# Two slabs on the unnormalised input open each hybrid layer, and the bias tables move ahead of the first layer

## The chip, the cores and the metric

The kernel runs on one core of a Trainium2 chip. The metric is device time in microseconds (us) of one launch; the number that counts is the median over several runs. One execution was also recorded by the hardware profiler, and every row below comes from that execution. TensorE is called PE, VectorE DVE, ScalarE ACT, SyncE SP; SP issues most of the loads and computes nothing.

## What is computed

The program is two blocks over 256 tokens of width 1024. The first block has two hybrid layers (convolution, retention and windowed attention side by side), the second has two layers of a mixer and a mixture of experts. The change touches the openings of the two hybrid layers and one table of the mixers. What matters of the reference:

```python
def hybrid_layer(x, positions, norm_g, w_in, ...):
    h = rms_norm(x, norm_g)                  # x * rsqrt(mean(x*x) + EPS) * norm_g
    z = h @ w_in
    (c_glu, c_gate, r_q, r_k, r_v, r_gate, a_q, a_k, a_v, a_gate, g_logit) = jnp.split(z, offsets, axis=-1)
    y_conv = conv_module(c_glu, c_gate, ...) @ w_conv_out   # v = a * sigmoid(b); 31 taps; layer norm
    ...
def sliding_window_attention(q, k, v, sink, rel_bias):      # in the mixers
    bias = rel_bias.astype(jnp.float32)[t5_causal_bucket(dist)]
    logits = jnp.where(mask[None, :, None, None], logits + bias, NEG_INF)
```

The factor rsqrt(mean(x*x) + EPS) belongs to a token. It can therefore be multiplied into a product after the matrix multiplication: (x * norm_g) @ w, times the token's factor, equals h @ w.

## The kernel before

**Numbers in two parts.** Every large product is made of three passes in a fast 32-bit format. Each operand is split into a rounded part (hi, made by ACT) and the rest (lo, made by DVE), and PE adds hi*hi, hi*lo and lo*hi. `split` (L87) does this for activations and for weights.

**Slabs.** Weights come in slabs of 1024 x 256 numbers, 1 MB each. `half` (L101) loads half a slab (512 KB) on SP's queue into `raw`, and splits it into `hi` and `lo`; there are 4 raw, 5 hi and 5 lo buffers. One slab feeds 48 matmuls of 256 columns: `mm_T` (L118) with the weights stationary, `mm_R` (L129) with the activations stationary. In the trace both orders run on lines L125 to L127 or L135 to L137.

**Opening of a hybrid layer.** `Norm` (L174) first makes u = x * norm_g in two parts (`uh`, `ul`) and the sums of squares, then in `_end` (L202) the reciprocal root `rinv` (a chain of small DVE instructions, spread over the partitions by PE on L151), and then, for each of eight blocks kt of 128 channels, h = x * norm_g * rinv on DVE (L212), its hi part `h_hi` on ACT and its lo part `h_lo` on DVE (L88). The first slab of the layer does not wait for h: `conv_unit(c, uu)` (L402) multiplies u by the slab and applies `rinv` to the result (L406). How many slabs do this is `UNORM[l]`. Then comes the slab of the attention keys, "ak", on h (L573), then "av" and the rest in the order of `HYB_ORDER`. Convolution unit c needs one slab and then 31 DVE instructions (taps), which `after_slab` (L380) hands out, 3.5 for each slab; a new unit is started when the list of taps is empty.

**Hold.** When h for kt = 7 is traced, `_end` remembers the ACT and the DVE instruction (L221). Of the half slabs traced after it, numbers 5 to 12 have their splits put behind these two instructions on ACT and DVE (L107 to L110, `HOLD` = 2); numbers 1 to 4 have not.

**Bias tables.** `toeplitz` (L303) makes the eight rows of relative bias for the mixers: it loads `relb`, `oneh` and `outw` on SP, and for each head runs a matmul of 32 rows x 383 columns (L312, two passes), one DVE instruction (L314) and one store to `tb_dram`, issued by ACT (L315). It takes both buffers of ring S, three of ring O and the two banks "sc". The mixers read the stored rows after the hybrid layers. In the order of layer 0 it is the letter t, behind the retention projection R.

**The planner.** The kernel's text sets priorities, not the order itself. A planner simulates the program and gives each engine its list: at each step the ready instruction of the highest priority, which is the one traced earlier; `high_priority` moves the marked ones ahead. Each engine then runs its list strictly in that order, and a waiting instruction holds all that stand behind it.

Of the kernel before, what the change touches and what calls it, by code (L numbers as in the profile page):

```python
# [26 lines left out]
RET_H = 4  # L27
LEAD = 420
HYB_BUFS = {"A": 3, "Q": 4, "S": 2, "V": 1, "B": 2, "O": 3, "G": 2, "H": 2, "W": 1, "X": 3, "Y": 2}
HYB_ORDER = ("aaraarArrnRtggggC", "aaraarArrnRtggggC")  # L30
MIX_ORDER = "tKQRv012uh3b"
HOIST, P_FIRST = True, 2
PEER_NS, PEER_NI, AHEAD = 44, 12, 2
UNORM = (1, 1)
MIX_U, PEER_U = 1, 1
BANKS = {"mm": (0, 1, 2), "sc": (3, 4), "tr": (5, 6), "o": (7,), "xo": (7,), "xm": (0, 1, 2, 7), "pm": (0, 1), "g": (3, 4), "gy": (3, 4), "acc": (2, 5, 6, 7), "pb": (2,)}
PEER_ADA = (1, 4)
# [13 lines left out]
def two_blocks_kernel(ctx: ExitStack, tc: tile.TileContext, ins: dict, out: bass.AP, stages=None):  # L51
# [6 lines left out]
    def const(name, shape, dt=F32, src=None, pool=glob):  # L58
        t = pool.tile(shape, dt, tag=name, name=name, bufs=1)
        nc.sync.dma_start(t, ins[name] if src is None else src)  # L60
        return t
# [21 lines left out]
    def nm(base):  # L83
        uid[0] += 1
        return f"{base}_{uid[0]}"
# [7 lines left out]
    def bank(ring="mm", shape=(P, 2, T)):  # L93
        n = turns[ring] = turns.get(ring, -1) + 1
        b = BANKS[ring][n % len(BANKS[ring])]
        return psum.tile(list(shape), F32, tag=f"bank{b}", name=nm(ring))
# [156 lines left out]
    stages_m = [l for k, l in stages if k == "m"]  # L253
# [12 lines left out]
    ada = {l: [] for l in mods}  # L266
# [15 lines left out]
    def ada_units(l, pool, tag, bufs, size, place=None):  # L282
        cact = []

        def load():
            cp, ct = place or (pool, "c_rows")
            cact.append(cp.tile([P, D], F32, tag=ct, name=nm("c_rows"), bufs=1))
            nc.sync.dma_start(cact[0], ins["c_rows"])
            nc.scalar.activation(cact[0], cact[0], AF.Silu)

        yield load
        for j in range(48):
            for c in range(0, D, size):
                def unit(j=j, c=c):
                    w = pool.tile([P, size], F32, tag=tag, name=nm("ada"), bufs=bufs)
                    nc.sync.dma_start(w, ins["w_ada"][l, j, :, c:c + size])
                    t = pool.tile([P, 1], F32, tag="adt", name=nm("adt"))
                    nc.vector.scalar_tensor_tensor(w, w, 1.0, cact[0][:, c:c + size], op0=ALU.mult, op1=ALU.mult,  # L298
                                                   accum_out=t)
                    nc.vector.tensor_tensor(mods[l][:, j:j + 1], mods[l][:, j:j + 1], t, op=ALU.add)  # L300
                yield unit

    def toeplitz(pool):  # L303
        relb = pool.tile([P, 1024], F32, tag="S", name="relb", bufs=2)[:32].rearrange("p (h c) -> p h c", h=8)
        ow = pool.tile([P, 1024], F32, tag="S", name="ow", bufs=2)
        oneh, outw = ow[:32, 0:383], ow[:, 512:895]
        nc.sync.dma_start(relb, ins["relb"])
        nc.sync.dma_start(oneh, ins["oneh"])
        nc.sync.dma_start(outw, ins["outw"])
        for h in range(8):  # L310
            pb = bank("sc", (P, 512))
            nc.tensor.matmul(pb[:, :383], relb[:, h, :], oneh, start=True, stop=True)  # L312
            row = pool.tile([P, 512], F32, tag="O", name=nm("row"), bufs=3)
            nc.vector.scalar_tensor_tensor(row[:, :383], pb[:, :383], 8.0, outw, op0=ALU.mult, op1=ALU.add)  # L314
            nc.scalar.dma_start(tb_dram[h], row[:, :383])  # L315

    def first_block(layers, following):
        with ExitStack() as bx:
            cp = bx.enter_context(tc.tile_pool(name="b1c", bufs=1))
            wk = bx.enter_context(tc.tile_pool(name="b1w", bufs=2))  # L320
            cst = {n: const(n, shape, pool=cp) for n, shape in (
                ("cos_r", [P, T]), ("sin_r", [P, T]), ("dist_f", [P, 2, T]), ("dist_b", [P, 2, T]),
                ("mask1", [P, 2, T]), ("rope_c", [P, 2, 16]), ("rope_s", [P, 2, 16]))}
            for l in stages_m[:1]:
                ada[l].extend(ada_units(l, wk, "S", 2, D))
            norm = Norm(stages[0], "tr", lambda: wk.tile([P, 2, T], F32, tag="X", name=nm("nx"), bufs=3))
            for k2 in range(KT // 2):
                norm.acc(k2)
            u = norm.end()
            for i, l in enumerate(layers):  # L330
                u = hybrid(l, wk, cst, u, following[i], i == 0 and stages_m, ada.get(i, []))
            if stages_m and not layers:
                toeplitz(wk)
            for a in ada.values():
                while a:
                    a.pop(0)()
        return u

    def hybrid(l, wk, cst, uu, follow, toep, ada):
        def cc(name, shape):  # L340
            t = wk.tile(shape, F32, tag=name, name=nm(name), bufs=1)
            nc.sync.dma_start(t, ins[name][l])
            return t
# [20 lines left out]
        for i, g in enumerate((qgr, kgr)):  # L364
            pair = []
            for n in ("rope_c", "rope_s"):
                t = wk.tile([P, 2, 16], F32, tag=f"{n}{i}", name=nm("rp"), bufs=1)
# [34 lines left out]
        def conv_unit(c, act=None):  # L402
            p = z(f"cv{c}", act=act)
            if act:
                zr = tl("X")
                nc.vector.tensor_tensor(zr, p, rbc, op=ALU.mult)  # L406
                p = zr
            sg = wk.tile([P, T], F32, tag="sg", name=nm("sg"))
            nc.scalar.activation(sg, p[:, 1, :], AF.Sigmoid)
            v = wk.tile([P, T + 30], F32, tag="cv", name=nm("cv"), bufs=2)  # L410
            nc.gpsimd.memset(v[:, :15], 0.0)
            nc.gpsimd.memset(v[:, T + 15:], 0.0)
            nc.vector.tensor_tensor(v[:, 15:T + 15], p[:, 0, :], sg, op=ALU.mult)
            a = conv[:, c, :]

            def tap(k):
                if k == 0:
                    nc.vector.tensor_scalar(a, v[:, :T], dw[:, c, 0:1], cb[:, c:c + 1], op0=ALU.mult, op1=ALU.add)
                else:
                    nc.vector.scalar_tensor_tensor(a, v[:, k:k + T], dw[:, c, k:k + 1], a, op0=ALU.mult, op1=ALU.add)  # L420
            taps.extend([lambda k=k: tap(k) for k in range(31)])
# [147 lines left out]

        for c in range(UNORM[l]):  # L570
            conv_unit(convs.pop(0), uu)
# [8 lines left out]
        def attn_s(s):  # L580
            qT = qk_R(f"aq{s}", ropes[0], qgc, tl("Q"))
            gate = silu_gate(f"ag{s}", "G")
            for k in range(2):
                attn_pair(s, k, qT, kT, va, gate)
            split(aop[0][:, 2 * s:2 * s + 2, :], aop[1][:, 2 * s:2 * s + 2, :], gate)
# [64 lines left out]
        def gated():  # L650
            if not cop:
                cop.extend(operand())
            s = count["g"]
            g = silu_gate(f"cg{s}")
            nc.vector.tensor_tensor(g, g, conv[:, 2 * s:2 * s + 2, :], op=ALU.mult)
            split(cop[0][:, 2 * s:2 * s + 2, :], cop[1][:, 2 * s:2 * s + 2, :], g)

        count = {t: 0 for t in HYB_ORDER[l]}
        for t in HYB_ORDER[l]:
            if t == "a":  # L660
                attn_s(count[t])
            elif t == "r":
                ret_head(count[t])
            elif t == "g":
                gated()
            elif t == "n":
                conv_norm()
            elif t == "t":
                if toep:
                    toeplitz(wk)  # L670
            else:
                project(*{"A": ("w_attn_out", [aop], 2), "R": ("w_ret_out", rops, 1), "C": ("w_conv_out", [cop], 0)}[t])
            count[t] += 1
# [530 lines left out]
    follows = list(stages[1:]) + [None]  # L1204
    nh = len(h_layers)
    u = first_block(h_layers, follows)
    for i in range(nh, len(stages)):
        k, l = stages[i]
        u = (mix if k == "m" else peer)(l, u, follows[i])
# [147 lines left out]
```

## Time and profile before

| | |
|---|---|
| median of three runs | 2998.45 us (2991.92 to 3002.57) |
| profiled execution | 3006.2 us, of which the span of instructions is 3004.3 us |
| granted PE clock, mean over the span | 0.98 of full |
| hybrid layer 0 opens | at 0 us; its second slab, "ak", ends at about 40 us |
| hybrid layer 1 opens | its second slab, "ak", ends at about 574 us |

Times in rows are counted from the start of the span. A row of the timeline gives the start, the duration, the engine and line, the operation, output and inputs, how many of them were merged, and in brackets how long the engine stood idle before it and what ended that. SPq and ACTq are issues of loads and stores on the queues of SP and ACT. Matmuls overlap, so their pitch (start to start) is their cost and not their duration.

### The profile page before, as it was taken

What the parts mean: (1) busy time and instruction counts of PE and PEld (TensorE: products, weight loads), DVE (VectorE), ACT (ScalarE), POOL (GpSimd) and SP (SyncE); (2) the same over time, 40 slices, a digit from 0 to 9 for tenths busy, and PEclk for the clock granted to TensorE, in tenths of its full rate; (3) what the DMA queues carried; (4) which work ended last, traced back from release to release, by engine and by line L of the source; (5) the groups of instructions that cost most, each with busy time, mean ns of one, the idle gap of its engine ahead of it and who ended that gap; (6) DMA issues with size and microseconds to landing.
All of it is one profiled execution on the core that took longest, in us unless ns stands there. A gap on an engine that the chain in (4) does not pass through costs nothing.

```text
span 3004.3 us, 55646 instructions
## 1 busy us (share of the span) xinstructions
PE 2936.9 (98%) x21784; PEld 2728.8 (91%) x21784; DVE 2421.5 (81%) x5084; ACT 1523.1 (51%) x2113; POOL 76.2 (3%) x92
## 2 busy tenths in 40 slices
PE   8999999999999999999999999999999999999999
PEld 8889999988999997999998779898899999888998
DVE  7889988788999677999976997767699996676665
ACT  5664545566454555464544444445455455444443
POOL 0000000000000000000000000000000000000000
PEclk8999999999999999999999999999899999999999
DMA  6357557434755453456767888864245676776664
GB/s 203 127 164 269 166 178 261 161 129 143 264 175 169 157 171 101 163 180 197 221 218 239 304 306 290 267 234 159 92 161 178 201 217 212 240 256 236 204 220 136
DMA packets 227064, 598.59 MB, mean 199 GB/s; under 512 B 24880, under 2 KB 85840, under 8 KB 223472
## 3 DMA queue, kind: packets, MB, share of 16 engines
q1 hardware_dynamic: 163824, 560.90, 55.9%
q10 hardware_dynamic: 62976, 34.13, 3.9%
q8 instruction: 171, 2.80, 0.4%
q14 instruction: 93, 0.76, 0.1%
HBM read 562.97 MB, written 31.98 MB: 198 GB/s over the span
## 4 chain that ended last, share of the span: by engine, by line
PE 63%; DMA 6%; DVE 5%; issue 2%; ACT 1%; DVEq 0%; ACTq 0%
PE acc L1186 17%; PE pm L125 8%; PE pm L126 8%; PE pm L127 8%; DMA ada<-in_w_ada_dram 5%; PE g L1119 3%; PE mm L125 3%; PE mm L127 3%; PE mm L126 3%; DVE lo L88 1%; DVE ada L298 1%; PE mm L136 1%; PE mm L137 1%; PE mm L135 1%; PE tr L144 1%
## 5 line engine op out<-in xcount | busy, mean ns | idle before, releaser
L88 ACT CAST hi<-raw 128x1024 fp32r<-128x1024 f32 x904 | 946.9, 1051 | 973.8 <-PE pm L126 245.6
L88 DVE TENSOR_TENSOR lo<-raw,hi 128x1024 fp32r<-128x1024 f32 x904 | 1117.7, 1238 | 280.9 <-ACT hi L88 277.8
L125 PE MATMUL pm<-h_hi,hi 128*128 128x256 f32 x2272 | 642.3, 283 | 9.5 <-ACT acti L972 6.4
L126 PE MATMUL pm<-h_lo,hi 128*128 128x256 f32 x2272 | 640.4, 282 | 4.5 <-DVE h_lo L219 4.5
L127 PE MATMUL pm<-h_hi,lo 128*128 128x256 f32 x2272 | 640.2, 282 | 1.3 <-DVE lo L88 1.3
L125 PEld LDWEIGHTS pm<-h_hi,hi 128*128 128x128 f32 x2272 | 430.0, 189 | 11.9 <-ACT acti L972 6.8
L126 PEld LDWEIGHTS pm<-h_lo,hi 128*128 128x128 f32 x2272 | 430.3, 189 | 6.4 <-DVE h_lo L219 4.9
L127 PEld LDWEIGHTS pm<-h_hi,lo 128*128 128x128 f32 x2272 | 430.1, 189 | 2.6 <-DVE lo L88 2.6
L125 PE MATMUL mm<-h_hi,hi 128*128 128x256 f32 x1472 | 419.6, 285 | 0.0
L126 PE MATMUL mm<-h_lo,hi 128*128 128x256 f32 x1472 | 416.0, 283 | 0.0
L127 PE MATMUL mm<-h_hi,lo 128*128 128x256 f32 x1472 | 415.6, 282 | 0.0
L1186 PE MATMUL acc<-hi,wal 128*128 128x512 f32 x1024 | 317.4, 391 | 4.8 <-DVE wal L88 4.7
L1186 PE MATMUL acc<-lo,wah 128*128 128x512 f32 x1024 | 316.5, 390 | 3.9 <-DVE lo L88 3.9
L1186 PE MATMUL acc<-hi,wah 128*128 128x512 f32 x1024 | 316.4, 390 | 0.0
L125 PEld LDWEIGHTS mm<-h_hi,hi 128*128 128x128 f32 x1472 | 278.6, 189 | 8.9 <-issue 8.3
L126 PEld LDWEIGHTS mm<-h_lo,hi 128*128 128x128 f32 x1472 | 278.6, 189 | 6.2 <-issue 6.1
L127 PEld LDWEIGHTS mm<-h_hi,lo 128*128 128x128 f32 x1472 | 278.4, 189 | 5.6 <-issue 5.6
L420 DVE SCALAR_TENSOR_TENSOR conv<-cv,conv_dw,conv 128x256 f32<-128x256 f32 x480 | 241.4, 514 | 3.3
L1186 PEld LDWEIGHTS acc<-hi,wal 128*128 128x128 f32 x1024 | 191.9, 188 | 48.2 <-DVE wal L88 8.4
L1186 PEld LDWEIGHTS acc<-lo,wah 128*128 128x128 f32 x1024 | 192.3, 188 | 45.6 <-DVE lo L88 5.1
L1186 PEld LDWEIGHTS acc<-hi,wah 128*128 128x128 f32 x1024 | 189.7, 188 | 37.3
L298 DVE SCALAR_TENSOR_TENSOR ada<-ada,c_rows 128x512 f32<-128x512 f32 (+1 forms) x144 | 127.0, 884 | 70.0 <-DMA ada<-in_w_ada_dram 65.8
(400 smaller groups left out, 4750.3 us busy)
## 6 DMA issues: line engine op xcount, KB each, us to landing
raw<-in_w_in_dram SPq DMA_DIRECT2D x264, 512.0 KB, 3.9
raw<-in_down_dram SPq DMA_DIRECT2D x256, 512.0 KB, 4.3
raw<-in_up_dram SPq DMA_DIRECT2D x256, 512.0 KB, 4.7
gd<-stg ACTq DMA_DIRECT2D x32, 832.0 KB, 5.0
gt<-gd SPq DMA_DIRECT2D x26, 1024.0 KB, 8.2
ada<-in_w_ada_dram SPq DMA_DIRECT2D x48, 512.0 KB, 5.0
ada<-in_w_ada_dram SPq DMA_DIRECT2D x96, 256.0 KB, 4.6
raw<-in_w_ret_out_dram SPq DMA_DIRECT2D x32, 512.0 KB, 3.6
```

The costliest lines, as they stand in the source:

```text
L88: return nc.scalar.copy(hi, src), nc.vector.tensor_tensor(lo, src, hi.bitcast(F32), op=ALU.subtract)
L125: nc.tensor.matmul(ps[:, ct, :], wh[:, kt, c], ah[:, kt, :], start=s, stop=False)
L126: nc.tensor.matmul(ps[:, ct, :], wh[:, kt, c], al[:, kt, :], start=False, stop=False)
L127: nc.tensor.matmul(ps[:, ct, :], wl[:, kt, c], ah[:, kt, :], start=False, stop=e)
L135: nc.tensor.matmul(ps[:, tt, :], ah[:, kt, c], wh[:, kt % 4, :], start=kt == 0, stop=False)
L136: nc.tensor.matmul(ps[:, tt, :], ah[:, kt, c], wl[:, kt % 4, :], start=False, stop=False)
L137: nc.tensor.matmul(ps[:, tt, :], al[:, kt, c], wh[:, kt % 4, :], start=False, stop=kt == KT - 1)
L144: nc.tensor.matmul(ps, sq[:, k, tt * P:(tt + 1) * P], ones_d[:, 0:1], start=start and k == 0, stop=stop and k == 1)
L298: nc.vector.scalar_tensor_tensor(w, w, 1.0, cact[0][:, c:c + size], op0=ALU.mult, op1=ALU.mult, accum_out=t)
L420: nc.vector.scalar_tensor_tensor(a, v[:, k:k + T], dw[:, c, k:k + 1], a, op0=ALU.mult, op1=ALU.add)
L1119: nc.tensor.matmul(pg[:, k, :], oh[0][:, j // 2, :, j % 2], oh[2 + i][:, j // 2, :, j % 2], start=i == 0, stop=i == 2)
L1186: nc.tensor.matmul(accs[2 * tt + n], lh[:, k, tsl], rh[k][:, n * 512:(n + 1) * 512], start=first and i == 0, stop=end and i == 2)
```

## The change

`UNORM` becomes (2, 2): in both hybrid layers the slabs of convolution units 0 and 1 run on u. The table step is taken out of the layer's order, and `toeplitz` is called once, after the opening norm and before the first hybrid layer is traced.

```diff
-HYB_ORDER = ("aaraarArrnRtggggC", "aaraarArrnRtggggC")
+HYB_ORDER = ("aaraarArrnRggggC", "aaraarArrnRggggC")
-UNORM = (1, 1)
+UNORM = (2, 2)
             u = norm.end()
+            if stages_m:
+                toeplitz(wk)
             for i, l in enumerate(layers):
-                u = hybrid(l, wk, cst, u, following[i], i == 0 and stages_m, ada.get(i, []))
-            if stages_m and not layers:
-                toeplitz(wk)
+                u = hybrid(l, wk, cst, u, following[i], ada.get(i, []))
-    def hybrid(l, wk, cst, uu, follow, toep, ada):
+    def hybrid(l, wk, cst, uu, follow, ada):
-            elif t == "t":
-                if toep:
-                    toeplitz(wk)
```

The loop that `UNORM` counts is unchanged: `for c in range(UNORM[l]): conv_unit(convs.pop(0), uu); after_slab()`.

## Rows read from the trace of the kernel before

**Rows 1.** The page's busy times: us (share of the span) and instructions.
```profile
PE 2936.9 (98%) x21784; PEld 2728.8 (91%) x21784; DVE 2421.5 (81%) x5084; ACT 1523.1 (51%) x2113; POOL 76.2 (3%) x92
```

**Rows 2.** Windows: busy us of PE, PEld, DVE, ACT, POOL; clock, DMA share, GB/s.
```profile
20.00:25.00 5.00, 1.97 (x9) 1.58 (x10) 4.36 (x13) 2.39 (x6) 0.00 (x0) 0.78 1.00 354
25.00:30.00 5.00, 3.02 (x15) 2.72 (x13) 0.86 (x3) 0.21 (x1) 0.00 (x0) 0.50 0.29 57
30.00:35.00 5.00, 1.85 (x5) 1.27 (x6) 2.72 (x10) 3.57 (x5) 0.00 (x0) 0.50 0.38 112
35.00:40.00 5.00, 5.00 (x26) 5.00 (x26) 3.92 (x4) 4.95 (x6) 0.00 (x0) 0.51 0.41 141
```

**Rows 3.** Timeline of PE at the opening of layer 0.
```profile
19.21 0.28 PE L126 MATMUL mm<-ul,hi 128*128 128x256 f32 x1
19.33 0.28 PE L127 MATMUL mm<-uh,lo 128*128 128x256 f32 x1
...
22.36 0.38 PE L135 MATMUL mm<-hi,h_hi 128*128 128x256 f32 x1 [1.47 <-ACT h_hi L88]
...
24.62 0.41 PE L135 MATMUL mm<-hi,h_hi 128*128 128x256 f32 x1
24.83 0.41 PE L136 MATMUL mm<-lo,h_hi 128*128 128x256 f32 x1
```

**Rows 4.** Timeline of DVE in the same stretch.
```profile
30.05 0.19 DVE L368 TENSOR_TENSOR rp<-rope_c,qg_row 128x32 f32<-128x32 f32 x1 [4.19 <-DMA qg_row<-in_qg_row_dram]
...
34.50 0.43 DVE L88 TENSOR_TENSOR h_lo<-nx,h_hi 128x256 fp32r<-128x256 f32 x1 [2.15 <-ACT h_hi L88]
35.45 3.50 DVE L88 TENSOR_TENSOR lo<-raw,hi 128x1024 fp32r<-128x1024 f32 x3 [0.52 <-ACT hi L88]
```

**Rows 5.** Timeline of ACT in the same stretch.
```profile
33.12 1.06 ACT L289 ACTIVATE c_rows<-c_rows 128x1024 f32<-128x1024 f32 x1 [0.74 <-DMA c_rows<-in_c_rows_dram]
...
34.38 2.94 ACT L88 CAST hi<-raw 128x1024 fp32r<-128x1024 f32 x3
...
40.43 0.59 ACT L242 COPY qn<-mm 128x512 f32<-128x512 f32 x1 [0.45 <-PE mm L137]
```

**Rows 6.** Timeline of SP's queue in the same stretch.
```profile
22.14 0.33 SPq L342 DMA_DIRECT2D b_gate<-in_b_gate_dram  x1
...
28.07 0.43 SPq L342 DMA_DIRECT2D qg_row<-in_qg_row_dram  x1
```

**Rows 7.** Timeline at the opening of layer 1, all engines.
```profile
562.42 0.60 PE L151 MATMUL tr<-X,ones_d 128*128 128x128 f32 x4
...
566.38 0.58 PE L137 MATMUL mm<-hi,h_lo 128*128 128x256 f32 x1 [1.37 <-DVE h_lo L88]
...
568.71 0.69 DVE L406 TENSOR_TENSOR X<-mm,rinv 128x512 f32<-128x512 f32 x1
...
570.21 3.50 DVE L88 TENSOR_TENSOR lo<-raw,hi 128x1024 fp32r<-128x1024 f32 x3 [0.15 <-ACT hi L88]
...
572.30 0.31 PE L137 MATMUL mm<-hi,h_lo 128*128 128x256 f32 x1
...
574.78 0.59 ACT L242 COPY qn<-mm 128x512 f32<-128x512 f32 x1 [0.33 <-PE mm L137]
```

**Rows 8.** Groups by line, 20 to 1090 us: count, busy us, mean ns, idle before.
```profile
L312 PE MATMUL sc<-ow,relb 32*128 32x383 f32 x16 | 8.1, 613 | 0.0
...
L314 DVE SCALAR_TENSOR_TENSOR row<-sc,ow 128x383 f32<-128x383 f32 x8 | 4.2, 549 | 2.9 <-PE sc L312 2.9
```

**Rows 9.** Timeline of PE: table matmuls in the layer's convolution norm.
```profile
453.63 2.92 PE L312 MATMUL sc<-ow,relb 32*128 32x383 f32 x4
...
460.81 1.55 PE L312 MATMUL sc<-ow,relb 32*128 32x383 f32 x4
```

**Rows 10.** Stores of the table rows (line 315), from issue to landing.
```profile
DMA to landing us min/median/max: 2.3/3.5/6.5
```

**Rows 11.** Window in the convolution norm of layer 0.
```profile
450.00:460.00 10.00, 10.00 (x38) 8.09 (x38) 6.26 (x19) 1.04 (x1) 1.26 (x1) 0.51 0.24 80
```

## The prediction

> **What bounds the kernel now.** I read the page's busy times first: PE is busy for 98% of the span [rows 1]. A change can then gain in two ways only: work that PE does in a full stretch is taken away, or a stretch where PE waits or runs at its half clock is filled. Next I read the windows of the opening. From 20 to 35 us PE is busy for 6.8 of 15 us, and its granted clock is 0.5 until 40 us, so 1.2 GHz in place of 2.4 [rows 2]. The timelines say why. The slab on u ends at about 19.5 us. Slab "ak" begins at 22.36 us [rows 3] and is over only at 40.4 us, where ACT fetches its result [rows 5]: 18 us. At the full pitch of 0.12 us (19.21 to 19.33) its 48 matmuls would take 5.8 us, at the half pitch of 0.21 us (24.62 to 24.83) 10.1 us [rows 3]. The rest is waiting for h. DVE stands 4.19 us at a small rope instruction whose constant `qg_row` arrives late, with the end of h queued behind it, and then 2.15 us for ACT [rows 4], which waited for `c_rows` [rows 5]. In layer 1 the same opening goes better: "ak" takes from about 563.0 to 574.4 us [rows 7], with PE at the half pitch from 566.4 to 572.3 us. The two openings hold some 12 and 5.6 us that are not work.
>
> **The change part by part**, against the profiled execution's own 3006.2 us (span 3004.3 and 1.9 around it).
>
> *a. The tables leave layer 0's full stretch.* They are 16 passes on PE, busy 8.1 us, with no idle time before them [rows 8]. Four passes took 1.55 us at the full clock and 2.92 us at the half clock [rows 9]; with 12 of the 16 at full clock that is 3 x 1.55 + 2.92 = 7.6 us. PE has no gap there, so the term is -7.6; its bounds are -6.2 (16 passes at the full clock) and -8.1.
>
> *b. The tables at the opening.* Eight rows again cost 6.2 us of PE, 4.2 us of DVE [rows 8] and eight stores issued on ACT's queue (an issue takes 0.33 us on SP's [rows 6]), plus three loads on SP. PE's cover is the time between the end of the second slab on u and the start of "ak", 26.6 to about 37 us (part c). The rows go through three buffers of ring O, each free again when its store has landed. A round is 0.55 + 0.33 + 3.5 = 4.4 us [rows 6, 8, 10], so the rows come as 3, 3 and 2, and if the first matmul has its loads at about 27 us the last two rows come at about 36 us, where PE has its work again: 2 x 0.78 = +1.6. Bounds: 0 (all covered) and +6.2 (none).
>
> *c. Opening of layer 0.* Unit 1's slab fills PE from the spread at about 20.9 us to 26.6 us; its four half slabs are not held, and before "ak" used the same four buffers in time. That takes 5.8 us out of the later full stretch. But now "ak" owns half slabs 5 and 6, and these are held behind the last part of h. The first lo of the three held ones ends at 35.45 + 1.2 = 36.6 us [rows 4]: "ak" can start there and not at 22.4. On SP the three new loads are traced ahead of the layer's constants. The nine issues from `b_gate` to `qg_row` have eight steps in 5.93 us, 0.74 each [rows 6], so `qg_row` may come 2.2 us later; ACT's wait for `c_rows` overlaps part of that, and I take 1.1. "ak" starts at 37.7 us. It then needs between 5.8 and 10.1 us; I take 7, because the full clock came back some 5 us after the end of h before (34.9 to 40 us [rows 2, 4]), and the table matmuls now shorten that wait. It ends at 44.7, 4.3 us later than before, with 5.8 us of work saved: -1.5. Bounds: 36.6 + 2.2 + 10.1 = 48.9 us, +2.7; and, if the planner's new order frees DVE and ACT of the two waits (4.19 + 2.15), a start at 30.3 and an end at 36.1 us, -10.1.
>
> The Trainium skill speaks against this placement: in "Trainium Kernel Development and Optimization", section Key Constraints, it says that loads from all issuing queues run on the same 16 DMA engines and interleave. The trace agrees that there is no room, with a DMA share of 1.00 at 354 GB/s from 20 to 25 us [rows 2]; the three loads are 376 KB, so by that rule all that follows comes 1.1 us later, and the sum would be 1.1 us worse if part c had not already taken as much from SP's steps.
>
> *d. Opening of layer 1.* Unit 1's slab runs from 563.0 (the spread, 562.42 + 0.60) to 568.8 us. The first held lo, now that of "ak", ends at 570.21 + 1.2 = 571.4 us [rows 7]. PE so trades two short waits for one of 2.6 us; "ak" then takes 5.8 us, or, if the clock falls as it did for 5.9 us, 28 matmuls at half pitch and 20 at full, 8.3 us. It ends at 577.2 to 579.7 against 574.4 us, with 5.8 us saved: -3.0 to -0.5, and I take -1.8, the middle.
>
> *e. Two more multiplications by rinv* on DVE, 0.69 us each [rows 7], stand beside matmuls and I cost them nothing: between 25 and 35 us DVE is busy 3.6 of 10 us [rows 2]. Without that cover they cost 1.4 us in all. The taps come in the same rhythm, since unit 1 would start after nine slabs anyway. What a new order by the planner does elsewhere the trace can't show; the nearest row is the convolution norm of layer 0, where PE ran at 0.51 clock for 10 us [rows 11] and so lost some 5 us. If that stretch is lost again or doubled, the sum moves by 5 us either way; I take 0.
>
> Sum: -7.6 + 1.6 - 1.5 - 1.8 = -9.3 us. The median of the runs lies 7.7 us under the profiled execution; 2998.45 - 9.3 = 2989 us.
>
> **The rivals.** *The openings stay as long as they are* (the change fills little). The hold moves with the slabs: "ak" waits where PE waited before. With c at +1, d at -0.5 and the tables' rows mostly among busy matmuls (b at +5), the sum is -2: 2996 us. For it speaks that the held splits end at 36.6 and 571.4 us whatever PE does before; against it, that 10 us of idle PE lie in front of the first.
>
> *The end of h comes free.* The DVE wait for `qg_row` rests on where the planner put one rope instruction. In layer 1, with its constants there, nothing of the kind is seen. If it goes, c is -10.1 and the sum -17.9: 2980.5 us. Against it: something new, a table row, can stand in the same place.
>
> *Slower: table rows stand ahead of the end of h.* They have priority over all of the layer except h and the slabs' splits, and the planner slips ready work into gaps, as it did with the rope instruction. If rows stand in front of h's last blocks on DVE, and their stores on ACT, h waits for two rounds of ring O and the first loads. At the median landing that is 2 x 4.4, at the largest, 6.5 us [rows 10], 2 x 7.4, and about 4 more for the loads. The loss eats all gains (7.6 without b's cost, 1.8, and the 1.5 of c) from 10.9 us on; with the full 18.8 us the result is +7.9: 3006 us. Against it: h's instructions are marked with the higher priority, so only a simulated gap lets rows through.
>
> **How the numbers follow.** Forecast 0.48, with an own range of 2984 to 2994 us; openings unchanged 0.26; end of h free 0.15; slower 0.11. A measurement here can tell about 0.3%, 9 us, from no change; so faster is below 2989.5 and slower above 3007.4 us. The forecast lies on the lower bound: 0.27 of its 0.48 is faster, with 0.15 from the freed h and 0.03 from unchanged openings with a luckier clock: 0.45. Slower has 0.08 of its rival (when landings are near their largest and the clock adds its 5 us) and 0.04 from an unlucky clock in the others: 0.12. Same: 0.43. The range reaches from the freed h with 4 us of better clock, 2976, to the slower rival's middle, 3005.
>
> **What would show it.** In the new profile: no line 312 after 100 us; its 16 passes between 25 and 40 us (b), with rows in threes. On PE, 96 matmuls on uh and ul back to back at both openings, then a wait that ends with the lo of a held split, not with h. "ak" over at about 45 and 578 us. If PE waits at about 30 us for h with a row of line 314 before it on DVE, the slower rival is at work; if "ak" begins near 30 us, the freed one. The prediction is wrong if the layer's later stretches, 50 to 540 us, change by more than the 5.8 + 7.6 us moved out of them.

## The result, and the profile after

The changed kernel takes 3023.66 us (median of six runs, 3012.6 to 3028.23), the kernel before 2993.81 us in the six runs beside it. The ratio is 1.0088, with an interval of 1.0071 to 1.0106. It is slower, by some 26 us by the ratio (30 us between these two medians); 2989 us was forecast. One execution of a run further down (the hold moved by one slab) took 10096.78 us, in a slow state, and is left out of that run's median. The profiled execution of before (3006.2 us) lies above that kernel's median and that of after (3012.6 us) below it, so the difference of the two profiles is too small by some 20 us; each kernel was therefore profiled a second time, with spans of 2992.9 and 3019.9 us, which lie near the medians. Sums below are made with this second pair, and rows are shown from the first profile of after, where the same things stand.

The page's busy times of after answer [rows 1]:

```profile
PE 2926.6 (97%) x21784; PEld 2720.0 (90%) x21784; DVE 2416.4 (80%) x5086; ACT 1520.2 (50%) x2111; POOL 81.2 (3%) x92
```

The work is the same to the instruction on PE. Its busy time is 10.3 us less than before in the first pair of profiles and 5.4 us more in the second (2935.1 against 2929.7 us), so it says nothing by itself. What has grown in both pairs is PE's idle time: from 67 to 84 us in the first and from 63 to 85 us in the second.

To find where, I cut each profiled execution at the start of four instructions: ACT's copy `qn` at the end of "ak" in layer 0, the last eight sums of the norm that opens layer 1 (line 144), the same copy in layer 1, and the first matmul of the first mixer (line 228). "Due" is what the moved work alone would change: a slab of 5.8 us goes from the middle into each opening, and 7.6 us of tables leave the middle.

| stretch, us | before, 2nd profile | after, 2nd profile | change | due | forecast |
|---|---|---|---|---|---|
| start to end of "ak", layer 0 | 39.86 | 51.21 | +11.4 | +5.8 and the tables | +5.9 |
| to the last sums of layer 1's norm | 512.31 | 523.17 | +10.9 | -13.4 | -13.4 |
| to the end of "ak", layer 1 | 15.57 | 24.80 | +9.2 | +5.8 | +4.0 |
| to the first mixer | 512.09 | 501.66 | -10.4 | -5.8 | -5.8 |
| rest | 1913.07 | 1919.06 | +6.0 | 0 | 0 |

The changes add up to the +27.0 us between the spans. The forecast's +5.9 is 4.3 of its part c and 1.6 of its part b. The largest miss by far is the second line, 24.3 us, in a stretch from which work was only taken away. I call this stretch the middle. The last line says little: over all 14 profiles of this study the rest lies between 1906.1 and 1919.1 us, with up to 6.5 us between two executions of one kernel.

The middle scatters too: in the first pair of profiles it takes 517.5 and 519.7 us, which makes its miss 15.6 us in place of 24.3. A good part of the scatter is a stretch at half clock around the convolution norm that comes and goes between executions of one kernel: from 440 to 460 us the clock was 0.74 in the first profile of before and 0.91 in the second, and from 460 to 480 us it was 1.00 in the first of after and 0.74 in the second. At 0.74 a window of 20 us loses some 5 us (20 x 0.26, an estimate). So the size of this miss is 15 to 25 us, and what has to be explained is what both profiles of after share.

**The middle.** Windows of after from 340 to 420 us (busy us of PE, PEld, DVE, ACT, POOL, then clock, DMA share, GB/s):

```profile
340.00:360.00 20.00, 17.71 (x136) 17.33 (x135) 20.00 (x41) 11.25 (x15) 3.96 (x3) 0.91 0.67 219
360.00:380.00 20.00, 17.11 (x122) 15.00 (x121) 20.00 (x50) 8.94 (x11) 0.15 (x2) 1.00 0.63 205
380.00:400.00 20.00, 16.80 (x135) 15.75 (x133) 19.47 (x58) 9.21 (x12) 0.16 (x2) 1.00 0.37 122
400.00:420.00 20.00, 16.94 (x112) 16.10 (x112) 20.00 (x48) 6.65 (x8) 1.13 (x3) 0.74 0.18 61
```

The same windows of before:

```profile
340.00:360.00 20.00, 20.00 (x157) 19.03 (x156) 17.42 (x27) 12.47 (x15) 0.00 (x0) 1.00 0.60 196
360.00:380.00 20.00, 20.00 (x160) 18.85 (x159) 18.96 (x60) 9.25 (x12) 0.00 (x0) 1.00 0.47 153
380.00:400.00 20.00, 20.00 (x160) 18.62 (x159) 18.74 (x36) 7.03 (x10) 0.16 (x2) 1.00 0.44 144
400.00:420.00 20.00, 20.00 (x172) 20.00 (x171) 19.98 (x30) 9.55 (x13) 3.93 (x2) 1.00 0.63 210
```

Before, PE has no gap here and runs at the full clock. After, DVE is the full engine, PE stands idle for 11.4 of 80 us, and in two windows, one with the longest gap, its clock is 0.91 and 0.74, which costs some 7 us more (20 x 0.35, an estimate). The second profile of after has 11.0 us of idle time and clocks of 0.91, 0.98 and 0.77 there. The waits of PE in this stretch (engine and line, what ended the wait, us in total, times, longest) are all for work that comes from DVE, and the largest is for a retention head:

```profile
PE tr L643 <- ACT O L635: 5.6, 2, 5.4
PE mm L125 <- DVE cv L413: 1.8, 1, 1.8
PE mm L136 <- DVE lo L88: 1.8, 1, 1.8
```

ACT's output of the head (line 635) itself waited 5.01 us for a chain of small DVE instructions, and these stood in DVE's queue between convolution taps:

```profile
401.43 1.64 ACT L635 ACTIVATE O<-sc,nb,rs 128x512 f32<-128x512 f32 x2 [5.01 <-DVE nb L633]
```

What fills DVE is a piece of background work that the change does not touch. The mixers' modulation rows (line 298, 48 DVE multiplications of 128 x 1024, each with a load of 512 KB from `w_ada`) go through ring S, the two buffers that the bias tables take for `relb` and `ow`. DVE's busy time on line 298 alone, in before:

```profile
260.00:280.00 20.00, 3.70 (x6) 1.00 0.85 281
280.00:300.00 20.00, 0.00 (x0) 1.00 0.49 166
...
340.00:360.00 20.00, 0.00 (x0) 1.00 0.60 196
...
480.00:500.00 20.00, 7.38 (x12) 1.00 0.94 331
500.00:520.00 20.00, 8.51 (x11) 1.00 0.87 309
```

and in after:

```profile
260.00:280.00 20.00, 6.80 (x11) 1.00 0.93 341
280.00:300.00 20.00, 5.47 (x10) 1.00 0.90 308
300.00:320.00 20.00, 6.93 (x11) 1.00 0.87 289
320.00:340.00 20.00, 5.31 (x10) 1.00 0.85 290
340.00:360.00 20.00, 3.65 (x6) 0.91 0.67 219
...
480.00:500.00 20.00, 0.00 (x0) 1.00 0.63 210
```

In before the modulation stops at about 270 us, when the load of `relb` takes its buffer (SP's queue), and goes on at 474 us, when the last table row is made (DVE):

```profile
266.66 0.34 SPq L307 DMA_DIRECT2D relb<-in_relb_dram  x1
```
```profile
469.36 0.56 DVE L314 SCALAR_TENSOR_TENSOR row<-sc,ow 128x383 f32<-128x383 f32 x1 [0.71 <-PE sc L312]
474.05 1.22 DVE L298 SCALAR_TENSOR_TENSOR ada<-ada,c_rows 128x1024 f32<-128x1024 f32 x1 [0.35 <-DMA ada<-in_w_ada_dram]
```

DVE has slack around there (12.4 of 20 us busy from 440 to 460 us). In after nothing holds ring S, and 21.4 us of DVE work run on through 280 to 360 us, where DVE has little to spare: in before it is busy for 17.4 to 20.0 us of each of the 20 us windows from 280 to 420 us. The last multiplication starts at 351.95 us, but DVE stays full to 420 us, and there the waits of PE lie. That it is still behind with its other work by then is argued from these windows; that the modulation puts it there is tested below.

**The opening of layer 0** in after. Windows that answer [rows 2]:

```profile
25.00:30.00 5.00, 1.70 (x7) 1.19 (x7) 1.14 (x4) 0.00 (x0) 0.00 (x0) 0.83 0.44 102
30.00:35.00 5.00, 1.75 (x3) 0.33 (x1) 2.23 (x10) 1.79 (x3) 0.00 (x0) 0.50 0.41 105
35.00:40.00 5.00, 4.46 (x7) 1.89 (x7) 4.49 (x9) 4.20 (x6) 0.00 (x0) 0.50 0.39 129
40.00:45.00 5.00, 5.00 (x22) 4.46 (x22) 4.66 (x7) 4.26 (x6) 0.00 (x0) 0.50 0.81 261
```

PE, DVE and ACT there, as in [rows 3 to 5]:

```profile
25.29 0.28 PE L127 MATMUL mm<-uh,lo 128*128 128x256 f32 x1
28.86 2.89 PE L312 MATMUL sc<-ow,relb 32*128 32x383 f32 x4 [3.30 <-DMA ow<-in_oneh_dram]
35.09 2.92 PE L312 MATMUL sc<-ow,relb 32*128 32x383 f32 x4 [3.34 <-DVE row L314]
38.46 0.58 PE L135 MATMUL mm<-hi,h_hi 128*128 128x256 f32 x1 [0.45 <-ACT hi L88]
...
51.33 0.91 PE L312 MATMUL sc<-ow,relb 32*128 32x383 f32 x2
```
```profile
32.71 0.19 DVE L368 TENSOR_TENSOR rp<-rope_c,qg_row 128x32 f32<-128x32 f32 x1 [6.58 <-DMA qg_row<-in_qg_row_dram]
34.49 0.55 DVE L314 SCALAR_TENSOR_TENSOR row<-sc,ow 128x383 f32<-128x383 f32 x1
35.55 0.55 DVE L314 SCALAR_TENSOR_TENSOR row<-sc,ow 128x383 f32<-128x383 f32 x1
37.18 0.76 DVE L88 TENSOR_TENSOR h_lo<-nx,h_hi 128x256 fp32r<-128x256 f32 x2 [0.49 <-ACT h_hi L88]
```
```profile
51.73 0.58 ACT L242 COPY qn<-mm 128x512 f32<-128x512 f32 x1
```

The slabs on u end at 25.3 us, "ak" begins at 38.46 us and ends at 51.73 us. PE has two clusters of table passes in the gap and the other eight passes among the matmuls of "ak"; the wait for `qg_row` has grown from 4.19 to 6.58 us.

**The opening of layer 1**, which answers [rows 7]:

```profile
571.43 0.95 PE L144 MATMUL tr<-ones_d,X 128*128 128x1 f32 x8
...
578.32 0.60 PE L151 MATMUL tr<-X,ones_d 128*128 128x128 f32 x4
586.13 0.58 PE L135 MATMUL mm<-hi,h_hi 128*128 128x256 f32 x1 [5.66 <-ACT hi L88]
587.75 0.58 PE L136 MATMUL mm<-lo,h_hi 128*128 128x256 f32 x1 [1.03 <-DVE lo L88]
```
```profile
578.96 0.42 DVE L207 COPY rinv<-tr 128x256 f32<-128x256 f32 x1 [3.49 <-PE tr L151]
```

From the last sums to the spread of `rinv` it is 6.9 us, where before it was 4.5. In between PE runs matmuls of the second slab on u: its last matmul starts at 580.19 us, and counted back from there at the pitch of 0.12 us some 35 of its 48 stand ahead of the spread. The planner put them there, and DVE waits 3.49 us for the spread. Then PE runs out of work and waits 5.66 and 1.03 us for the split of "ak", held behind the end of h.

### The profile page after: what moved, and what is told of

Read it like the earlier page. It is cut to its first block, busy times and chain, and to the rows that moved or that the text cites. A ratio compares the mean times of both kernels' runs of the same rounds, so it can differ in the third digit from the quotient of the medians.

```text
span 3010.8 us, 55679 instructions
## 1 busy us (share of the span) xinstructions
PE 2926.6 (97%) x21784; PEld 2720.0 (90%) x21784; DVE 2416.4 (80%) x5086; ACT 1520.2 (50%) x2111; POOL 81.2 (3%) x92
## 4 chain that ended last, share of the span: by engine, by line
PE 82%; DVE 9%; DMA 5%; issue 2%; ACT 1%; SPq 0%; ACTq 0%; DVEq 0%
PE acc L1183 19%; PE pm L125 8%; PE pm L126 7%; PE pm L127 7%; PE mm L125 6%; PE mm L126 6%; PE mm L127 6%; DMA ada<-in_w_ada_dram 4%; PE g L1116 3%; DVE lo L88 3%; PE mm L135 2%; PE mm L136 2%; PE mm L137 2%; DVE ada L298 1%; PE tr L144 1%
## 5 line engine op out<-in xcount | busy, mean ns | idle before, releaser
L125 PE MATMUL mm<-h_hi,hi 128*128 128x256 f32 x1440 | 408.1, 283 | 2.1 <-DVE cv L413 1.8
L126 PE MATMUL mm<-h_lo,hi 128*128 128x256 f32 x1440 | 405.5, 282 | 0.0
L127 PE MATMUL mm<-h_hi,lo 128*128 128x256 f32 x1440 | 404.4, 281 | 0.2 <-DVE rs L165 0.2
L125 PEld LDWEIGHTS mm<-h_hi,hi 128*128 128x128 f32 x1440 | 270.8, 188 | 10.4 <-issue 6.4
L126 PEld LDWEIGHTS mm<-h_lo,hi 128*128 128x128 f32 x1440 | 270.8, 188 | 6.4 <-issue 6.3
L127 PEld LDWEIGHTS mm<-h_hi,lo 128*128 128x128 f32 x1440 | 270.4, 188 | 4.5 <-issue 4.0
L420 DVE SCALAR_TENSOR_TENSOR conv<-cv,conv_dw,conv 128x256 f32<-128x256 f32 x480 | 228.2, 496 | 1.7
L135 PE MATMUL mm<-hi,h_hi 128*128 128x256 f32 x576 | 167.2, 291 | 8.2 <-ACT hi L88 6.1
```

The source lines that it names most:

```text
L125: nc.tensor.matmul(ps[:, ct, :], wh[:, kt, c], ah[:, kt, :], start=s, stop=False)
L126: nc.tensor.matmul(ps[:, ct, :], wh[:, kt, c], al[:, kt, :], start=False, stop=False)
L127: nc.tensor.matmul(ps[:, ct, :], wl[:, kt, c], ah[:, kt, :], start=False, stop=e)
L135: nc.tensor.matmul(ps[:, tt, :], ah[:, kt, c], wh[:, kt % 4, :], start=kt == 0, stop=False)
```

## The experiments

The expectations name the theories by letters. Above all: S, the freed ring S lets the modulation run where DVE is full; O, the openings themselves cost it; L, the loads at the start; H, the hold; P, the place of the spread among the slabs. Ratios are to the kernel before, timed beside each run; a difference of two runs is taken from their ratios where nothing else is said. The profiled execution of a run can lie far from its median, and where that matters it is said.

**One half of the change each.** Tables only (after, with one slab on u):

```diff
-UNORM = (2, 2)
+UNORM = (1, 1)
```

> The tables at the opening, but one slab on u per layer as before (UNORM 1, 1). Theory S (the table tiles had held both buffers of ring S from 267 to 470 us and so kept the 49 modulation units, which use the same ring, out of the retention stretch; without them 20 to 30 units run at 270 to 350 us, where DVE is full): PE waits at 330 to 410 us as in the changed kernel, and the median is 10 to 25 us above before (ratio 1.003 to 1.008). Rival O (the two-slab openings cost the time): no waits at 330 to 410 us, ratio 0.997 to 1.000, since 7.6 us of PE leave a full stretch. Rival L (the three loads and eight rows at the start cost the time): the first 60 us are some 10 us longer net and the rest is as before, ratio 1.002 to 1.004.

Measured: 3005.56 us, 1.0031 [1.0014, 1.0047].

Slabs only (before, with two slabs on u):

```diff
-UNORM = (1, 1)
+UNORM = (2, 2)
```

> Two slabs on u per layer (UNORM 2, 2), the tables where they were. Theory S: the modulation units stay out of 280 to 460 us; no waits at 330 to 410 us; only the openings change (layer 1 loses some 3 us net, layer 0 between -2 and +3), so 2990 to 3002 us, ratio 0.998 to 1.003. Rival O: most of the loss is here, ratio 1.005 to 1.010. Rival L: as theory S.

Measured: 3008.85 us, 1.0048 [1.0032, 1.0064]. Each half alone is slower than before, by about 9 and 14 us, and together they make nearly the 26. So two causes are at work, and the profiles keep them apart. With the tables only, the middle takes 523.8 us, as in after, and the modulation on line 298 runs on to about 328 us; the opening of layer 1 takes 16.8 us, as in before, and that of layer 0 42.3 us, 2.4 more than in the second profile of before, so the loads at the start (theory L, 10 us) are not the cause. With the slabs only the modulation stops at 280 us, PE has no gap from 340 to 420 us, the middle takes 513.5 us and the opening of layer 1 25.8 us. Theory S had allowed the slabs alone no more than 1.003; that the openings cost time as well is its miss.

**The ring.** After, with the old place of the tables kept by two placeholder tiles in ring S, whose only use needs the convolution norm's result, so that they hold the ring until 465 us (in before the last table row is made at 469 us):

```diff
+HYB_ORDER = ("aaraarArrnRtggggC", "aaraarArrnRggggC")
...
+            elif t == "t":
+                for i in range(2):
+                    plug = wk.tile([P, 1024], F32, tag="S", name=nm("plug"), bufs=2)
+                    nc.gpsimd.memset(plug[:, 0:1], 0.0)
+                    nc.vector.tensor_tensor(plug[:, 0:1], plug[:, 0:1], conv[:, i, 0:1], op=ALU.add)
```

> The changed kernel with two placeholder tiles in ring S at the tables' old place, each written in one column by POOL and released by one tiny DVE instruction that needs the convolution norm's result; it holds ring S until about 470 us without any table work. Theory S: the modulation units run after 460 us again; 2990 to 3003 us, ratio 0.998 to 1.003, 15 to 30 us under the changed kernel. Rivals O and L: no gain over the changed kernel, 3020 to 3026 us, ratio 1.008 to 1.010.

Measured: 2998.6 us, 1.0013 [1.0001, 1.0026]. Two tiles that compute nothing take some 22 us off the changed kernel (25 us between the medians). The modulation on line 298 stops again, and PE in the windows of 340 to 420 us is as before, but for one gap:

```profile
280.00:300.00 20.00, 3.68 (x6) 1.00 0.74 247
300.00:320.00 20.00, 0.00 (x0) 1.00 0.59 195
...
480.00:500.00 20.00, 6.15 (x10) 1.00 0.90 317
```
```profile
340.00:360.00 20.00, 18.01 (x147) 17.60 (x147) 19.57 (x37) 13.02 (x18) 1.43 (x3) 1.00 0.55 184
360.00:380.00 20.00, 20.00 (x152) 18.09 (x151) 18.97 (x51) 10.14 (x11) 0.00 (x0) 1.00 0.49 159
380.00:400.00 20.00, 20.00 (x174) 20.00 (x173) 19.01 (x44) 10.10 (x15) 0.16 (x2) 1.00 0.48 159
400.00:420.00 20.00, 20.00 (x172) 20.00 (x171) 19.95 (x30) 8.68 (x10) 2.80 (x2) 1.00 0.53 184
```

The middle takes 506.0 us, 17.2 us less than in the second profile of after and 13.7 less than in the first. The openings are what they were in after, 51.7 and 25.3 us, so the gain is not there. The profiled execution is the fastest of its twelve (2991.3 us); its end behind the first mixer's start is the shortest of all profiles (1906.1 us), so its span is no measure of the gain.

The other way to hold the ring is to do the tables twice, early and at the old place:

```diff
+            elif t == "t":
+                if toep:
+                    toeplitz(wk)
```

> The changed kernel, and the tables computed a second time at their old place, which adds 16 passes, 6 to 8 us of PE in a full stretch, and holds ring S again. Theory S: faster than the changed kernel although it does more: 3000 to 3010 us, ratio 1.002 to 1.006, no PE waits of over 1 us at 340 to 410 us. Rivals O and L: as slow as the changed kernel and some 6 us more, 3028 us, ratio 1.010 to 1.012.

Measured: 3013.32 us, 1.0055 [1.0037, 1.0073]. With 7.6 us more work on PE than after it is still 10 us faster. Against the placeholder it is 14.7 us slower by the medians, more than 7.6; its middle (511.5 us) has 5.6 of this, and the rest lies behind the mixers' start, where profiles scatter. I can't say more of it.

The placeholder with one slab on u (the tables alone are early, and the ring is held):

```diff
-UNORM = (2, 2)
+UNORM = (1, 1)
```

> The tables at the opening and the placeholder in ring S, but one slab on u per layer (UNORM 1, 1): the run on early tables alone, plus the placeholder. Theory S: the modulation units are back after 460 us, so it lies 15 to 22 us under early tables alone (3005.6 us), at 2985 to 2991, ratio 0.996 to 0.998, as the effects add up (placeholder -22, second slab +14 in the runs so far). Rival N (the effects are accidents of each planned order and don't add): anywhere between 2990 and 3006 us.

Measured: 2995.7 us, 1.0000 [0.9988, 1.0012]; a gain was expected and did not come. The middle takes 504.9 us, 18.8 us less than with the tables only, so the ring's part is there a second time, without the slabs. Some 5 of the 18.8 us (20 x 0.26, an estimate) are the half clock around the convolution norm, which need not belong to it: from 440 to 480 us the clock was 0.85 and 0.89 in the run with tables only and 1.00 here. Against the second profile of before the middle is 7.4 us shorter, the opening of layer 0 takes 2.3 us more, that of layer 1 the same, and the first mixer begins 8.1 us earlier. The end comes 4.4 us earlier in this profile, which lies 5.4 us under the median of its runs, and no earlier by the ratio. So the tables' time does leave the middle; where the typical execution gives it back the profile doesn't show, and it stays open.

**The openings.** Slabs only, with the hold moved by one slab, so that both half slabs of "ak" are split when they arrive:

```diff
-HOLD, MARK = 2, 7
+HOLD, MARK = 3, 7
```

> Two slabs on u per layer, tables at the old place, HOLD 3 in place of 2, so that the splits of slab ak are not put behind the end of h. Theory H (the hold makes the 6.7 us PE wait at the opening of layer 1 and the one at 26 to 37 us): ak begins with the first blocks of h, PE waits at most 3 us at layer 1's opening; 8 to 12 us under the same kernel with HOLD 2 (3008.9 us). Rival P (the spread matmul of the norm, queued behind unit 1's slab on PE, makes h late): the wait at layer 1's opening stays over 4 us and the time within 4 us of 3008.9.

Measured: 3000.84 us, 1.0007 [0.9996, 1.0017]. Slabs only, with the second slab's matmuls put behind the spread:

```diff
         for c in range(UNORM[l]):
-            conv_unit(convs.pop(0), uu)
+            with ExitStack() as es:
+                if c:
+                    es.enter_context(tc.issue_after(spread_mm[0].ins))
+                conv_unit(convs.pop(0), uu)
```

> Two slabs on u per layer, tables at the old place, HOLD 2, and the matmuls of the second slab queued on PE behind the norm's spread matmuls. Theory H: h comes 3.5 us sooner at layer 1, but ak still waits for its held splits, so the wait is 3 us instead of 6.7: 2 to 4 us under 3008.9 us. Rival P: the wait at layer 1 is down to 1 to 3 us and most of the 14 us of loss goes, 2996 to 3001 us.

Measured: 2996.19 us, 0.9993 [0.9981, 1.0005]. Both edits:

> Both edits: HOLD 3, and the second slab's matmuls queued behind the spread. Theories H and P both expect that ak follows the second slab without a wait of more than 1 us at layer 1; layer 0 still waits for the constants in DVE's queue. The opening of layer 1 is then 5 to 6 us shorter net than before, 2990 to 2998 us, ratio 0.998 to 1.000. If it stays above 3004 us, the loss of the second slab is not at the openings at all (rival M: it is in the attention stretch at 60 to 120 and 620 to 650 us, where two units' taps crowd DVE).

Measured: 2988.76 us, 0.998 [0.9967, 0.9993]. Of the medians (3008.85 us with the slabs alone) the one edit takes back 8.0 and the other 12.7 us, and with both the slabs are a gain against before, of 0.2%. The openings follow: that of layer 1 goes from 25.8 us to 19.6 with the hold moved, 22.7 with the spread first and 17.6 with both, though it has a slab more in it than before (15.6 in the second profile of before); that of layer 0 goes from 46.8 us to 43.7, 46.1 and 39.7. For the second edit alone the two openings make only 3.8 of the 12.7 us; its profiled execution is the slowest of its runs (3007.65 us), and where the others win the rest is not shown. PE and DVE in layer 1, with both edits:

```profile
548.97 0.95 PE L144 MATMUL tr<-ones_d,X 128*128 128x1 f32 x8
554.24 0.71 PE L153 MATMUL tr<-X,ones_d 128*128 128x128 f32 x4 [0.62 <-DVE X L152]
560.53 0.28 PE L135 MATMUL mm<-hi,h_hi 128*128 128x256 f32 x1
```
```profile
554.99 0.42 DVE L209 COPY rinv<-tr 128x256 f32<-128x256 f32 x1 [0.61 <-PE tr L153]
```

The wait of 3.49 us for the spread (now line 153) is 0.61 us, and "ak" starts with no wait for a split.

On top of these edits I tried to free layer 0's opening of its late constants, with `ret_decay`, `qg_row` and `kg_row` loaded early on ACT's queue, and `c_rows` activated behind h:

```diff
+        with tc.high_priority(offset=LEAD + 100):
+            rdec = cc("ret_decay", [P, 8], nc.scalar)
+            qgr = cc("qg_row", [P, 16], nc.scalar)
+            kgr = cc("kg_row", [P, 16], nc.scalar)
```

> The kernel with both opening edits (spread first, HOLD 3; tables at the old place), and besides the loads of ret_decay, qg_row and kg_row issued early on ACT's queue, and c_rows' SiLU queued on ACT behind h's last block. Theory C (what still makes PE wait at 23 to 31 us is the constants at the head of DVE's and ACT's queues): h is complete at about 29 us, PE waits under 2 us in 20 to 40 us, 2 to 5 us under the kernel without it (2988.8), ratio 0.996 to 0.998. Rival: h's own chain on DVE (8 products, 8 lo parts, the drains) is the limit, nothing is gained, 0.998 again.

Measured: 2998.49 us, 1.0003 [0.9988, 1.0018]: a miss. With the two edits alone DVE no longer waits for `qg_row`, because h is later and its rope instruction too (31.68 us), so there was less to win than thought; and "ak" now ends at 43.3 us and not at 39.7. The spread that feeds h comes later (PE):

```profile
25.89 1.22 PE L153 MATMUL tr<-nx,ones_d 128*128 128x128 f32 x4 [6.67 <-DVE nx L152]
```

In the kernel without this edit it stands at 24.16 us. ACT, with the loads now on its queue, had waited 3.61 us for another load, `conv_w`, just before. So the opening is 3.6 us longer. The medians are 9.7 us apart, but the two profiled executions, each the fastest of its runs, only 0.9 us, so where the typical execution loses the rest stays open.

**All of it.** Both slabs on u with the two edits, the tables early, and the placeholder at their old place:

> Everything of the change, mended: two slabs on u, tables at the opening, with the placeholder in ring S, HOLD 3 and the second slab queued behind the spread. If the 7.6 us of table passes taken out of the full stretch are worth something once the rest is mended, 2979 to 2986 us, ratio 0.995 to 0.997; if they are given back at the opening, as the run on tables and placeholder with one slab (ratio 1.000) says, it is as the same kernel with the tables at the old place, 2988 to 2994 us, ratio 0.998 to 1.000.

Measured: 2986.88 us (2983.12 to 2993.89), 0.997 [0.9958, 0.9982]. It beats both kernels, by the medians the one before by 9 us (0.3%) and the changed one by 37 us. That the early tables add to it is not shown: its interval overlaps that of the same kernel without them (0.998), and what they save in the middle (506.8 against 509.3 us) is less than they cost in the opening (45.8 against 39.7 us).

**Both kernels again**, unchanged, for the second profiles:

> The kernel before once more, for a second trace of it: the first profiled execution lies 9 us above the median of its runs, and this one is to show which waits and half-clock stretches of the first were of that execution alone. All theories: 2990 to 3003 us, the same order of instructions; the openings at 22 to 40 and 563 to 574 us as before, no modulation units between 280 and 460 us.

> The changed kernel once more, for a second trace: the first profiled execution is the fastest of its runs. Theory S: the waits of PE at 340 to 410 us (11 us in the first trace) are there again, and so is the 6.7 us wait at layer 1's opening, 3018 to 3030 us. If the waits at 340 to 410 us are gone and the time is still above 3015 us, ring S isn't the cause.

Measured: 2994.67 us (span 2992.9) and 3021.7 us (span 3019.9). What the first profile of after shows is there again: 3.49 us of DVE's wait for the spread, 5.66 and 1.04 us of PE's for the splits of "ak" in layer 1, line 298 busy from 280 to 360 us, and PE idle for 11.0 us between 340 and 420 us. In before, PE has 80.0 us of 80 there.

## Why the prediction was wrong

The forecast was a gain of 9.3 us. By its own steps:

*a, the tables leave the middle, -7.6:* right as an amount of work. With one slab on u and the ring held the middle is 7.4 us shorter than in the second profile of before (12.6 than in the first, which lost some 5 us to the half clock there). Without the ring held it is more than lost.

*b, the tables at the opening, +1.6 (0 to 6.2):* +2.3 us with one slab on u, but 6.1 us between the two kernels with both slabs and edits, at the upper bound, and 4.9 us between the slabs alone (46.8) and after (51.7). The first cluster started about where it was placed, but only eight passes ran in the gap, at the half clock in the second cluster (2.92 us) and in the first profile in the first as well (2.89 us, in the second profile 1.52), and eight fell among busy matmuls instead of four.

*c, opening of layer 0, -1.5:* the mechanism was right, and the start of "ak" too: 36.09 us with the slabs alone and 38.46 us in after, against 37.7 us. `qg_row` ended DVE's wait 2.7 us later than before (32.71 against 30.05 us), close to the 2.2 us worked out, of which only 1.1 were counted. The length of "ak" was mis-sized. I took 7 us; with the slabs alone it took 10.7 us, which makes the term +1.1 (46.8 - 39.9 - 5.8). The table matmuls in front of "ak" did not bring the full clock back sooner, as I had assumed: from 40 to 45 us it was 0.50 and 0.58 in the two profiles of after, and 0.71 with the slabs alone. The opening came out at +11.4 us where c and b gave 5.9.

*d, opening of layer 1, -1.8:* the sign was wrong. The opening grew by 9.2 us, so with 5.8 us of work taken away later the term is +3.4. I let the second slab run behind the spread. It ran in front of it, and so h, and with it the held split of "ak", came later: the wait was 5.66 + 1.03 us and not 2.6. This and the hold are shown as causes by the edits that remove them.

*e, the planner's new order elsewhere, taken as 0 with 5 us either way:* this is the step that failed, by 24.3 us in the middle (15.6 by the first pair of profiles). I bounded it by a stretch of half clock around the convolution norm. That stretch does come and go by some 5 us, but it is not the loss; I did not ask what the moved step had kept out. It was in sight: the tables are said to take both buffers of ring S, and the load of `relb` is issued at 266.66 us, 187 us before the matmuls of [rows 9]. (These are not the first: in the same profile of before four of the sixteen passes run from 383.31 us on, and the last row is made at 469.36 us.) Nothing else that uses this ring ran in between. The freed ring let 21.4 us of modulation into a stretch where DVE was full, and PE lost 11 us of waiting and some 7 us of clock there. The placeholder's 22 us show this cause, and its part in the middle with one slab on u shows it again; the tables computed twice, which hold the ring with real work, go the same way. The condition that the prediction set for being wrong, a change of the stretch from 50 to 540 us beyond the 13.4 us moved out, is what happened.

The rival with unchanged openings had the sizes right for layer 0 (c at +1 and b at +5, where +1.1 and 4.9 were measured with both slabs), but not for layer 1 (-0.5, where it was +3.4), and it said nothing of the middle. The rival on the slower side named another place: table rows ahead of the end of h on DVE. Two rows do stand there, at 34.49 and 35.55 us, but they cost 1.1 us; that rival was right in sign and not in cause. The freed end of h did not come; the wait for `qg_row` grew from 4.19 to 6.58 us.

What gave something back was the stretch of layer 1 behind its opening, -10.4 us where 5.8 were due. With one slab and early tables, where nothing was due, it is -8.5 us, and with the placeholder added -3.3. That looks like a gain from the modulation being done early, but with two slabs the placeholder changes nothing there (500.4 us against 501.7 in after), so I can't divide it and its cause stays open.

## What to carry to other kernels

When a step moves, ask not only what it does but what it holds: a buffer ring that it occupies may be the only thing that keeps background work out of a full stretch. So look, for every ring in the diff, at who else uses it and when these users run in the trace. And a slab that is independent of a chain is a filler only behind the chain's small instructions; where a planner may put it in front of them, tie it behind them, and move along with it whatever counts slabs.
